# The fifth group of a down projection by seven products, and a reordered tail

## The chip, the cores and the metric

The kernel runs on one core of a Trainium2 chip. A core has a matrix engine (TensorE, in the profile PE, with its weight loads as PEld), a vector engine (DVE), a scalar engine (ACT), GpSimd (POOL) and SyncE (SP, which issues most DMAs). Each works through its own queue; they meet through semaphores. The metric is the time of one execution on the device in microseconds, the median of several runs.

## The reference

One encoder layer in float32, 512 rows of 1024 values. What bears on the change is its second half: a gated feed-forward part, whose down projection has a contraction of 2816 = 22 chunks of 128, and an embedding gate with a norm before and after it.

```python
    h2 = rmsnorm(x, norm_ffn_g[i])
    up = jnp.einsum('bsd,df->bsf', h2, w_up[i])
    up = causal_depthwise_conv(up, conv_w[i], conv_b[i])
    act = jax.nn.gelu(up[..., :D_FF]) * up[..., D_FF:]
    x = x + jnp.einsum('bsf,fd->bsd', act, w_down[i])

    h3 = rmsnorm(x, norm_ple_g[i])
    ple = jnp.einsum('bse,ed->bsd', p[i], w_ple[i])
    x = x + ple * jax.nn.sigmoid(jnp.einsum('bsd,de->bse', h3, w_ple_gate[i]))
return rmsnorm(x, norm_final_g)
```

## The kernel before

**Matmuls.** Every float32 product is made of three matmuls on float32r parts: an operand is split into a rounded high part and a low part (the rest), and low x high, high x low and high x high are summed in one PSUM bank. A matmul has a 128 x 128 stationary operand and a moving one of 128 x 512.

**Weights.** `load_w` (line 145) loads a piece of 512 KB into one of three raw buffers with a DMA from SP, casts it to the high part on ACT (line 153) and makes the low part in one of two ways: a subtraction on DVE (line 159), or, with "dma", a negated copy on ACT (line 156) and a DMA from GpSimd that adds the raw piece to it in place (line 157). The parts go to a ring of five pairs and one extra pair, so that a piece waits for the matmuls of the piece six before it. `split_w` (line 262) does the DVE way for weights that are in SBUF already.

**The up projection.** Eleven pairs of chunks, q = 0 to 10. For each, `up_jobs` (line 1332) has two jobs, gate and linear: 48 matmuls each, a convolution, the gelu or the product. The result goes to `done` (line 1437).

**The down projection by seven products.** Four chunks (two pairs q) make a group: 2 x 2 blocks of rows (256 each), of the contraction (256) and of columns (512), multiplied by seven products instead of eight. `pair_parts` (line 1311) makes the row-side operands of a pair, A11, A12, A22 and four sums S1 to S4, and their high and low parts, in a tile of one of the slots 2, 3, 5 and 7. `down_jobs(g)` (line 1367) loads the group's four weight blocks into slot 4, combines them in place, and makes the products in four jobs: A11 and S2; A12 and S1; S4 and S3; A22. Each product is 12 matmuls. Results are added to x1, the rows of the running sum, by DVE (line 1394); what A11 gives is needed in all four quarters and is gathered over the groups in `usum` (line 1401), and added to three quarters at the end (line 1467). `N_SEVEN` = 4 groups cover chunks 0 to 15.

**Order.** The list `jobs` alternates up jobs and down jobs; a job's weights are prepared while the job before it runs. The order in the text is binding for TensorE and SP in the sections marked `manual_schedule`; the other engines' order is set by a planner that runs through the program in simulated time and takes, of the instructions that are ready, the earlier one in the text.

**The last chunks and the tail.** Chunks 16 to 21 are projected plainly: the first column half for all four row blocks with six chunks (72 matmuls, line 1476), the second half block by block (`pd`, line 1538). As a block's second half ends, `evac_x2` (line 1480) adds it to x1, sums the squares and makes the norm: `rms_rows` (line 460) with a square root on ACT (line 391), four small DVE instructions and two scaled halves (line 468). `rest[rb]` then transposes that block (line 421) and splits it into h3T (lines 380, 381). The gate projection `pg` follows, 24 matmuls a block and column half, with its weights in pieces of two chunks. Two gain rows (lines 1472, 1473) go to slot 5 and the embedding rows `ple` (line 1477, 2 MB) to slot 4, when these are free. At the end `evac_gate` makes sigmoid, product, sum and the final norm, and the rows are stored.

Of the kernel before, what the change touches and what calls it, by code (L numbers as in the profile page):

```python
# [43 lines left out]
def hybrid_block(  # L44
# [217 lines left out]
    def split_w(raw):  # L262
        hi, lo = split_tiles(2, 512)
        A.copy(hi, raw)  # L264
        V.tensor_tensor(lo, raw, hi.bitcast(F32), ALU.subtract)  # L265
        return hi, lo
# [1038 lines left out]

    N_SEVEN = 4
    f_last, n_last = 4 * N_SEVEN, NF - 4 * N_SEVEN

    def pair_parts(e, o, t):
# [55 lines left out]
    def down_jobs(g):  # L1367
# [62 lines left out]

        def run3(ws):
            product(A22, ws[0], "z", add(2, 0))
        return [(ready0, run0), (ready1, run1), (ready2, run2), (lambda: (split_w(b21),), run3)]

    tiles = {}

    def done(q, i, uls):
        if q < 2 * N_SEVEN:
            if i:
                tiles[q] = slot((2, 3, 5, 7)[q % 4])  # L1440
                pair_parts(*uls, tiles[q])
            return
        if q == 2 * N_SEVEN and i == 0:
            tiles["last"] = tuple(k_view(slot(n), n_last) for n in (2, 3))
        split_out(tiles["last"], uls[i], (slice(None), 2 * q + i - f_last, slice(None)))

    jobs = up_jobs(0, done) + up_jobs(1, done)
    jobs[0] = (lambda: w_up0[0], jobs[0][1])
    jobs[1] = (lambda: w_up0[1], jobs[1][1])
    for g in range(N_SEVEN):  # L1450
        ups = up_jobs(2 * g + 2, done) + up_jobs(2 * g + 3, done)
        for pair in zip(ups, down_jobs(g)):
            jobs += pair
    jobs[2] = (lambda: up1, jobs[2][1])
    for q in range(2 * N_SEVEN + 2, NF // 2):
        jobs += up_jobs(q, done)

    with tc.manual_schedule(engines={ET.PE, ET.SP}):
        ws = jobs[0][0]()
        for n, (_, products) in enumerate(jobs):  # L1460
            nxt = jobs[n + 1][0]() if n + 1 < len(jobs) else None
            products(ws)
            ws = nxt
    for r in range(2):
        for rows, ch in ((0, 1), (2, 0), (2, 1)):
            t = x1[:, rows + r, 512 * ch:512 * ch + 512]
            V.tensor_tensor(t, t, usum[:, r, :], ALU.add)


    tail = slot(5, F32).rearrange("p (n c) -> p n c", n=4)  # L1470
    gple, gfin = tail[:, 0], tail[:, 1]
    nc.sync.dma_start(gple, rows_bc(norm_ple_g[0], D))
    nc.sync.dma_start(gfin, rows_bc(norm_final_g, D))
    ple = slot(4, F32).rearrange("p (b c) -> p b c", b=NB)
    f0, n, act = f_last, n_last, tiles["last"]
    proj_N(w_down_v, f0, n, act, 0, evac_x1a, rb_outer=False)
    nc.sync.dma_start(ple, ple_d.rearrange("(b q) c -> q b c", q=P))
    h3T = tuple(k_view(slot(i)) for i in (0, 1))

    def evac_x2(bk, rb, ch):  # L1480
        evac_x1(bk, rb, ch)
        ss1 = square_sum(bk, x1[:, rb, 512:], "s1")
        rest[rb] = rms_rows(x1[:, rb, :], half[rb], ss1, gple, scr, h3T, rb, tail[:, 2 + rb % 2])


    def add_ple(bk, rb, c):
# [47 lines left out]
            queue.dma_start(out_rows(rb, slice(0, D)), ple[:, rb, :])  # L1534
        rest[rb] = close

    with tc.manual_schedule(engines={mybir.EngineType.PE}):
        pd = proj_N_steps(w_down_v, f0, n, act, 1, evac_x2)
        steps(pd, 3 * n * 2 + 9)
        rest[0]()  # L1540
        steps(pd, 3 * n)
        rest[1]()
        steps(pd, 3 * n - 9)
        pg = proj_N_steps(w_pg_v, 0, NK, h3T, 0, evac_gate, subs=load_N(w_pg_v, 0, NK, 0, ("dma", "dma")))
        steps(pg, 20)
        rest[2]()
        steps(pg, 24)
        rest[3]()
        steps(pg, 52)
        subs = load_N(w_pg_v, 0, NK, 1, ("dma", "dma", None, None))  # L1550

# [60 lines left out]
```

## Time and profile before

| what | value |
|---|---|
| time, median of 3 runs (lowest, highest) | 932.3 us (931.84, 932.31) |
| the profiled execution | 932.14 us |
| its span, first to last instruction | 930.0 us |
| granted TensorE clock, mean | 0.997 |
| PE busy | 919.0 us, 99% |
| DVE busy, ACT busy | 634.8 us (68%), 556.4 us (60%) |
| matmuls | 4375 |

A row of instructions in order of time has the start in us from the span's start, the duration, the engine, the line, the operation and the tiles (out<-in). A row of the groups by line has the count, the busy time in us and the mean in ns, and behind the second bar the idle time of the engine before it and what ended it. Matmuls overlap: each is recorded with 0.39 us, and one starts every 0.23 us. "Issue to landing" of a DMA is the time from its issue to the last of its semaphore updates.

### The profile page before, as it was taken

How to read it: one execution, taken by the hardware profiler on the slowest of the kernel's cores; microseconds unless marked ns; L12 is line 12 of the kernel's file. 1: busy time of each engine (PE TensorE's matmuls, PEld its weight loads, DVE VectorE, ACT ScalarE, POOL GpSimd, SP SyncE). 2: the span in 40 equal slices, each digit the busy share in tenths (PEclk: the TensorE clock that was granted, in tenths of full speed). 3: DMA queues.
4: the chain of work that ended last, by engine and by line, in shares of the span. 5: the costliest groups of instructions: out<-in, count | busy, mean ns of one | idle time of the engine just before them, and what ended most of it. 6: DMA issues, size and time to landing. Idle time of an engine off the chain costs nothing.

```text
span 930.0 us, 12122 instructions
## 1 busy us (share of the span) xinstructions
PE 919.0 (99%) x4375; PEld 766.9 (82%) x4375; DVE 634.8 (68%) x1157; ACT 556.4 (60%) x891; POOL 102.6 (11%) x153
## 2 busy tenths in 40 slices
PE   9999999999999999999999999999999999999996
PEld 7878888888888888888888998888888888888885
DVE  5786899568777776634696747867676677464654
ACT  7754675477666677536556575756564645545633
POOL 1000000400000011000111010111110101100124
PEclk9999999999999999999999999999999999999998
DMA  9533264656444466499766496795675774975422
GB/s 338 193 93 113 81 185 121 235 140 166 117 115 122 117 163 153 167 364 323 178 202 117 136 205 183 169 251 116 155 205 128 225 167 101 236 239 136 116 66 91
DMA packets 109367, 156.36 MB, mean 168 GB/s; under 512 B 6132, under 2 KB 71852, under 8 KB 109308
## 3 DMA queue, kind: packets, MB, share of 16 engines
q1 hardware_dynamic: 96380, 110.73, 36.7%
q0 software_dynamic: 12784, 44.34, 24.2%
q8 instruction: 34, 0.56, 0.2%
q10 hardware_dynamic: 144, 0.52, 0.1%
q14 instruction: 25, 0.20, 0.1%
HBM read 105.74 MB, written 12.62 MB: 127 GB/s over the span
## 4 chain that ended last, share of the span: by engine, by line
PE 96%; DMA 1%; ACT 1%; DVE 1%; issue 0%; SPq 0%; DVEq 0%; POOLq 0%
PE bank L181 18%; PE bank L183 18%; PE bank L185 18%; PE bank L1387 8%; PE bank L1197 4%; PE bank L313 3%; PE bank L320 3%; PE bank L317 3%; PE bank L245 3%; PE bank L247 3%; PE bank L243 3%; PE bank L905 2%; PE bank L896 2%; PE bank L168 2%; PE bank L169 2%; PE bank L167 2%
## 5 line engine op out<-in xcount | busy, mean ns | idle before, releaser
L181 PE MATMUL bank<-slot,wlo 128*128 128x512 f32 (+1 forms) x696 | 272.6, 393 | 0.0
L183 PE MATMUL bank<-slot,whi 128*128 128x512 f32 (+1 forms) x696 | 267.3, 384 | 0.0
L185 PE MATMUL bank<-slot,whi 128*128 128x512 f32 (+1 forms) x696 | 266.9, 384 | 0.0
L185 PEld LDWEIGHTS bank<-slot,whi 128*128 128x128 f32 x696 | 130.9, 188 | 25.2
L181 PEld LDWEIGHTS bank<-slot,wlo 128*128 128x128 f32 x696 | 130.9, 188 | 20.7
L183 PEld LDWEIGHTS bank<-slot,whi 128*128 128x128 f32 x696 | 131.3, 189 | 19.4
L153 ACT CAST whi<-raw 128x1024 fp32r<-128x1024 f32 x95 | 99.2, 1048 | 39.0 <-PE bank L185 13.5
L157 POOL DMA_DIRECT2D wlo<-raw x55 | 47.7, 868 | 532.0 <-ACT wlo L156 351.5
L159 DVE TENSOR_TENSOR wlo<-raw,whi 128x1024 fp32r<-128x1024 f32 x39 | 48.4, 1244 | 27.5 <-ACT whi L153 27.0
L156 ACT ACTIVATE wlo<-whi 128x1024 fp32r<-128x1024 f32 x55 | 58.0, 1059 | 1.0
L1387 PE MATMUL bank<-whi,slot 128*128 128x512 f32 x176 | 56.5, 389 | 0.0
L245 PE MATMUL bank<-wlo,slot 128*128 128x512 f32 x106 | 41.7, 393 | 0.3 <-DVE wlo L159 0.2
L243 PE MATMUL bank<-whi,slot 128*128 128x512 f32 x106 | 41.7, 394 | 0.0
L878 ACT ACTIVATE t<-t,mn 128x512 f32<-128x512 f32 (+1 forms) x64 | 35.8, 560 | 9.7 <-DVE mn L875 8.3
L247 PE MATMUL bank<-whi,slot 128*128 128x512 f32 x106 | 41.5, 392 | 0.0
L1300 DVE SCALAR_TENSOR_TENSOR ul<-bank,cvT,ul 128x511 f32<-128x511 f32 x22 | 16.5, 750 | 36.5 <-ACT ul L1299 36.5
L1387 PEld LDWEIGHTS bank<-whi,slot 128*128 128x128 f32 x176 | 33.0, 188 | 6.9
L264 ACT CAST whi<-slot 128x1024 fp32r<-128x1024 f32 x22 | 23.0, 1044 | 23.8 <-PE bank L185 11.6
L1299 ACT ACTIVATE ul<-bank,cvT 128x512 f32<-128x512 f32 x22 | 17.1, 776 | 32.6 <-PE bank L185 32.6
L1300 DVE SCALAR_TENSOR_TENSOR ug<-bank,cvT,ug 128x511 f32<-128x511 f32 x22 | 16.4, 747 | 26.7 <-ACT ug L1299 26.6
L265 DVE TENSOR_TENSOR wlo<-slot,whi 128x1024 fp32r<-128x1024 f32 x22 | 26.9, 1221 | 11.0 <-ACT whi L264 11.0
L1387 PE MATMUL bank<-wlo,slot 128*128 128x512 f32 x88 | 34.2, 389 | 0.0
(368 smaller groups left out, 1913.7 us busy)
## 6 DMA issues: line engine op xcount, KB each, us to landing
wlo<-raw POOLq DMA_DIRECT2D x55, 512.0 KB, 5.3
raw<-in_w_up_dram SPq DMA_DIRECT2D x44, 512.0 KB, 5.2
raw<-in_w_in_dram SPq DMA_DIRECT2D x36, 512.0 KB, 3.9
more<-in_w_in_dram SPq DMA_DIRECT2D x20, 512.0 KB, 6.9
slot<-in_w_down_dram SPq DMA_DIRECT2D x16, 512.0 KB, 6.3
raw<-in_w_branch_b_dram SPq DMA_DIRECT2D x8, 512.0 KB, 3.9
slot<-in_w_out_dram SPq DMA_DIRECT2D x4, 1024.0 KB, 9.4
raw<-in_w_branch_a_dram SPq DMA_DIRECT2D x8, 512.0 KB, 7.1
```

The lines of the kernel that those rows point to most:

```text
L153: A.copy(hi, raw)
L156: A.activation(lo, hi.bitcast(F32), AF.Copy, scale=-1.0)
L157: G.dma_start(lo, raw, accum_op=ALU.add)
L159: (sub or V).tensor_tensor(lo, raw, hi.bitcast(F32), ALU.subtract)
L181: T.matmul(out_ap, wl, ah, start=(n == 0 and k == 0), stop=False)
L183: T.matmul(out_ap, wh, al, start=False, stop=False)
L185: T.matmul(out_ap, wh, ah, start=False, stop=end)
L243: T.matmul(bk, alo[:, k, r], wh, start=(k == 0), stop=False)
L245: T.matmul(bk, ahi[:, k, r], wl, start=False, stop=False)
L247: T.matmul(bk, ahi[:, k, r], wh, start=False, stop=(k == nk - 1))
L1197: T.matmul(bk, l, m, start=(fresh and q == 0 and n == 0), stop=(q == 3 and n == 2), skip_group_check=not fresh)
L1387: T.matmul(bk, l, m, start=(fresh and k == 0 and n == 0), stop=(k == 1 and n == 2), skip_group_check=not fresh)
```

## The change

`N_SEVEN` becomes 5: chunks 16 to 19 are a fifth group, and two chunks, 20 and 21, are left for the plain projection. The fifth group's first two jobs alternate with the last up pair as in the other groups. Its second half goes into `last_rows`: S3 and S4 (they end the upper rows' sums), then the plain chunks of both column halves for row blocks 0 and 1, then A22 (which ends the lower rows' sums), then the plain chunks for blocks 2 and 3. S3 stands before S4, where it stood behind it. The norms are taken apart into `norm_y` (the factor) and `norm_x2` (the scaled rows); both factors of a row half stand before the first block's rows. A small activation loads the square root's table ahead. The plain chunks' weights now go the "dma" way, and so do three of the four gate pieces, which are prepared one by one between these steps; the fourth is subtracted on DVE. The last pair's parts are in slot 7. The gain rows' loads are now in the section in which SP's order is that of the text; the `ple` load stands behind `last_rows`. PSUM banks are named in turn by two short lists. Transposes of blocks 0 and 1 stand before and after the last six plain matmuls, those of blocks 2 and 3 after 22 and 44 gate matmuls (before: 20 and 44).

```diff
--- before.py
+++ after.py
@@ -1305,7 +1305,7 @@
-    N_SEVEN = 4
+    N_SEVEN = 5
     f_last, n_last = 4 * N_SEVEN, NF - 4 * N_SEVEN
 
     def pair_parts(e, o, t):
@@ -1430,9 +1430,19 @@
 
         def run3(ws):
             product(A22, ws[0], "z", add(2, 0))
+        if g == N_SEVEN - 1:
+
+            def rows01(ws):
+                product(S3, ws[1], "z", add(2, 1))
+                product(S4, ws[0], "y", add(0, 1))
+
+            def rows23(w):
+                product(A22, w, "z", add(2, 0))
+            end.update(ready=ready2, rows01=rows01, ready23=lambda: split_w(b21), rows23=rows23)
+            return [(ready0, run0), (ready1, run1)]
         return [(ready0, run0), (ready1, run1), (ready2, run2), (lambda: (split_w(b21),), run3)]
 
-    tiles = {}
+    tiles, end = {}, {}
 
     def done(q, i, uls):
         if q < 2 * N_SEVEN:
@@ -1441,46 +1451,92 @@
                 pair_parts(*uls, tiles[q])
             return
         if q == 2 * N_SEVEN and i == 0:
-            tiles["last"] = tuple(k_view(slot(n), n_last) for n in (2, 3))
+            t = slot(7)
+            tiles["last"] = k_view(t, n_last), k_view(t[:, 512 * n_last:], n_last)
         split_out(tiles["last"], uls[i], (slice(None), 2 * q + i - f_last, slice(None)))
 
     jobs = up_jobs(0, done) + up_jobs(1, done)
     jobs[0] = (lambda: w_up0[0], jobs[0][1])
     jobs[1] = (lambda: w_up0[1], jobs[1][1])
-    for g in range(N_SEVEN):
+    for g in range(N_SEVEN - 1):
         ups = up_jobs(2 * g + 2, done) + up_jobs(2 * g + 3, done)
         for pair in zip(ups, down_jobs(g)):
             jobs += pair
+    for pair in zip(up_jobs(2 * N_SEVEN, done), down_jobs(N_SEVEN - 1)):
+        jobs += pair
     jobs[2] = (lambda: up1, jobs[2][1])
-    for q in range(2 * N_SEVEN + 2, NF // 2):
-        jobs += up_jobs(q, done)
-
-    with tc.manual_schedule(engines={ET.PE, ET.SP}):
-        ws = jobs[0][0]()
-        for n, (_, products) in enumerate(jobs):
-            nxt = jobs[n + 1][0]() if n + 1 < len(jobs) else None
-            products(ws)
-            ws = nxt
-    for r in range(2):
-        for rows, ch in ((0, 1), (2, 0), (2, 1)):
+
+    f0, n = f_last, n_last
+    proj = [None, None]
+
+    def evac_x2(bk, rb, ch):
+        evac_x1(bk, rb, ch)
+        sums[rb] = square_sum(bk, x1[:, rb, 512:], "s1")
+
+    def norm_y(rb):
+        V.tensor_tensor(half[rb], half[rb], sums[rb], ALU.add)
+        return rstd_of(half[rb], 1.0 / D)
+
+    def norm_x2(rb, y):
+        hn = tail[:, 2 + rb % 2]
+        for c in (slice(0, 512), slice(512, D)):
+            V.scalar_tensor_tensor(hn[:, c], x1[:, rb, c], y, gple[:, c], ALU.mult, ALU.mult)
+        rest[rb] = lambda: transpose_split(hn, h3T, rb)
+
+    pg_w = []
+
+    def pg_weights(j, sub):
+        pg_w.append(load_w(w_pg_v[:, 2 * j:2 * j + 2, 0:512], 2, 512, sub))
+
+    def add_usum(rows, ch):
+        for r in range(2):
             t = x1[:, rows + r, 512 * ch:512 * ch + 512]
             V.tensor_tensor(t, t, usum[:, r, :], ALU.add)
 
-
-    tail = slot(5, F32).rearrange("p (n c) -> p n c", n=4)
-    gple, gfin = tail[:, 0], tail[:, 1]
-    nc.sync.dma_start(gple, rows_bc(norm_ple_g[0], D))
-    nc.sync.dma_start(gfin, rows_bc(norm_final_g, D))
-    ple = slot(4, F32).rearrange("p (b c) -> p b c", b=NB)
-    f0, n, act = f_last, n_last, tiles["last"]
-    proj_N(w_down_v, f0, n, act, 0, evac_x1a, rb_outer=False)
-    nc.sync.dma_start(ple, ple_d.rearrange("(b q) c -> q b c", q=P))
-    h3T = tuple(k_view(slot(i)) for i in (0, 1))
-
-    def evac_x2(bk, rb, ch):
-        evac_x1(bk, rb, ch)
-        ss1 = square_sum(bk, x1[:, rb, 512:], "s1")
-        rest[rb] = rms_rows(x1[:, rb, :], half[rb], ss1, gple, scr, h3T, rb, tail[:, 2 + rb % 2])
+    def last_rows(ws):
+
+        w23 = end["ready23"]()
+        for ch, evac in enumerate((evac_x1a, evac_x2)):
+            proj[ch] = proj_N_steps(w_down_v, f0, n, tiles["last"], ch, evac,
+                                      subs=load_N(w_down_v, f0, n, ch, ("dma",)))
+        pg_weights(0, "dma")
+
+        A.activation(epst2, usum[:, 1, 0:1], AF.Sqrt, scale=0.0, bias=epst)
+        end["rows01"](ws)
+        state["turn"], state["bank"] = ["mm", "sc"], 0
+        steps(proj[0], 6 * n)
+        pg_weights(1, "dma")
+        steps(proj[1], 6 * n)
+        ys = [norm_y(rb) for rb in range(2)]
+        norm_x2(0, ys[0])
+        end["rows23"](w23)
+        norm_x2(1, ys[1])
+        pg_weights(2, "dma")
+        state["turn"], state["bank"] = ["mm", "sc", "mm", "pt", "pt", "sc", "mm", "pt"], 0
+
+    jobs.append((lambda: end["ready"](), last_rows))
+
+
+    def run_jobs(ws, n0, n1):
+        for n in range(n0, n1):
+            nxt = jobs[n + 1][0]() if n + 1 < len(jobs) else None
+            jobs[n][1](ws)
+            ws = nxt
+        return ws
+
+    with tc.manual_schedule(engines={ET.PE, ET.SP}):
+        ws = run_jobs(jobs[0][0](), 0, len(jobs) - 1)
+        tail = slot(5, F32).rearrange("p (n c) -> p n c", n=4)
+        gple, gfin = tail[:, 0], tail[:, 1]
+        nc.sync.dma_start(gple, rows_bc(norm_ple_g[0], D))
+        nc.sync.dma_start(gfin, rows_bc(norm_final_g, D))
+        h3T = tuple(k_view(slot(i)) for i in (0, 1))
+    with tc.manual_schedule(engines={ET.PE}):
+        for rows, ch in ((0, 1), (2, 1), (2, 0)):
+            add_usum(rows, ch)
+        last_rows(ws)
+        ple = slot(4, F32).rearrange("p (b c) -> p b c", b=NB)
+        nc.sync.dma_start(ple, ple_d.rearrange("(b q) c -> q b c", q=P))
 
 
     def add_ple(bk, rb, c):
@@ -1534,18 +1590,23 @@
             queue.dma_start(out_rows(rb, slice(0, D)), ple[:, rb, :])
         rest[rb] = close
 
-    with tc.manual_schedule(engines={mybir.EngineType.PE}):
-        pd = proj_N_steps(w_down_v, f0, n, act, 1, evac_x2)
-        steps(pd, 3 * n * 2 + 9)
+    with tc.manual_schedule(engines={ET.PE}):
+        pg = proj_N_steps(w_pg_v, 0, NK, h3T, 0, evac_gate, subs=pg_w)
+        steps(proj[0], 6 * n)
+        steps(proj[1], 3 * n)
         rest[0]()
-        steps(pd, 3 * n)
+        steps(proj[1], 3 * n)
         rest[1]()
-        steps(pd, 3 * n - 9)
-        pg = proj_N_steps(w_pg_v, 0, NK, h3T, 0, evac_gate, subs=load_N(w_pg_v, 0, NK, 0, ("dma", "dma")))
-        steps(pg, 20)
+        state["turn"], state["bank"] = BANK_TURN, 1
+        ys = [norm_y(rb) for rb in (2, 3)]
+        norm_x2(2, ys[0])
+        pg_weights(3, None)
+        norm_x2(3, ys[1])
+        steps(pg, 22)
         rest[2]()
-        steps(pg, 24)
+        steps(pg, 22)
         rest[3]()
+    with tc.manual_schedule(engines={ET.PE}):
         steps(pg, 52)
         subs = load_N(w_pg_v, 0, NK, 1, ("dma", "dma", None, None))
 
```

## The prediction

> **What bounds the kernel now.** I read the page first (busy times, the chain by engine), then the chain of waits in order of time over the last 170 us, then busy time by stage, and last the engines' own order in time around the edit. The page's head and its chain:
>
> ```profile
> span 930.0 us, 12122 instructions
> PE 919.0 (99%) x4375; PEld 766.9 (82%) x4375; DVE 634.8 (68%) x1157; ACT 556.4 (60%) x891; POOL 102.6 (11%) x153
> PE 96%; DMA 1%; ACT 1%; DVE 1%; issue 0%; SPq 0%; DVEq 0%; POOLq 0%
> ```
>
> PE is busy for 99% and is 96% of the chain, so the kernel is as long as its matmuls, and what matters is how many there are and whether one of them ever waits. Busy time by stage (columns: stretch, its length, PE, PEld, DVE, ACT, POOL with counts, granted clock, DMA share, GB/s):
>
> ```profile
> 740.00:760.00 20.00, 20.00 (x90) 16.56 (x89) 15.21 (x22) 12.06 (x16) 3.37 (x4) 1.00 0.69 187
> 850.00:900.00 50.00, 49.92 (x237) 41.38 (x236) 26.72 (x52) 29.24 (x52) 9.69 (x11) 1.00 0.50 116
> 861.48:877.72 16.24, 16.24 (x81) 13.61 (x80) 10.85 (x28) 10.11 (x19) 0.86 (x1) 1.00 0.39 100
> 900.00:930.00 30.00, 21.48 (x118) 18.59 (x116) 12.74 (x34) 9.61 (x21) 12.77 (x28) 0.92 0.18 70
> ```
>
> In the loop of seven-product groups (740 to 760) PE never waits although DVE is busy for 15.2 of 20 us. In the tail, where the edit is, DVE has much room: 10.85 of 16.24 us between 861.48 and 877.72. The last 8 us are the final norm and store, which the edit doesn't touch. The chain of waits, start, length, what:
>
> ```profile
> 767.60 5.44 PE bank L1387 x24
> 783.92 5.44 PE bank L1387 x24
> 800.24 5.44 PE bank L1387 x24
> 816.56 2.72 PE bank L1387 x12
> 867.57 0.87 PE bank L421 x8
> 875.28 4.54 DMA wlo<-raw
> ```
>
> The first four rows are the fourth group: 84 matmuls, 5.44/24 = 0.2267 us each. From its end, 819.28, 96 up-projection matmuls, 72 of the first output half and 45 of the second put the first transposes at 819.28 + 213 x 0.2267 = 867.57, which is the fifth row to the hundredth: nothing waits there, and positions may be computed by counting. The last row is the one wait in the tail. PE's own rows there:
>
> ```profile
> 879.40 0.39 PE L243 MATMUL bank<-whi,slot 128*128 128x512 f32 x1
> 879.87 0.50 PE L245 MATMUL bank<-wlo,slot 128*128 128x512 f32 x1
> ```
>
> The second starts 0.47 after the first instead of 0.23: 0.24 us lost to the low part of the last gate weight piece.
>
> **The change part by part.**
>
> *Matmuls removed.* Chunks 16 to 19 of the down projection took 4 chunks x 4 row blocks x 2 halves x 3 terms = 96 matmuls; as a fifth group they take 7 x 2 x 2 x 3 = 84. Twelve fewer, all on the path: 12 x 0.2267 = **-2.72 us**. Everything else PE does (transposes, gate) keeps its count.
>
> *Position of the rest.* From 819.28: 96 + 48 matmuls of the last up projection and the group's first two steps, so S3 starts at 851.92; S4 ends at 857.36; plain chunks, rows 0 and 1: 860.08 and 862.80 (block 0 complete at 861.44, as before); A22 ends at 865.52; then two blocks to 868.24, block 2 to 869.60, transposes of block 0 (0.87), block 3 to 871.83, transposes of block 1 to 872.70, and the gate starts there. Its fourth weight piece is first read after 18 matmuls, 876.78, and the transposes of block 2 stand after 22, 877.69.
>
> *Parts at nothing.* The operands of tiles 8 and 9 are now built by the pair routine and its seven weight splits and four combinations, more DVE and ACT work in 819 to 852; the cover is the same as in the row 740 to 760, where that very pattern leaves PE at 20.00 of 20. S3 now follows S1 at once and needs a bank that the A12 eviction frees; A12 ends 2.72 us earlier and an eviction is 0.69 (below), so without cover at most 0.7. The Sqrt table load comes off block 0's chain; that buys slack, not time. The two gain loads stand in SP's order behind the last up loads and the four new loads; they waited for the fourth group's end before too and are needed some 45 us later:
>
> ```profile
> 800.14 0.37 SPq L1477 DMA_DIRECT2D slot<-ple_d  x1
> 811.44 0.37 SPq L150 DMA_DIRECT2D raw<-in_w_up_dram  x1
> 818.63 0.34 SPq L1472 DMA_DIRECT2D slot<-in_norm_ple_g_dram  x1
> ```
>
> The 2 MB ple load moves most: its slot now holds the fifth group's weights until the last of them is split. That split's buffer is released at 843.76 (three quarters through the last linear half), so with a cast of 1.05 and a subtraction of 1.24 the load can go from about 846.1. DMA rows for 800 to 820, when it ran before, and for 841 to 866:
>
> ```profile
> DMA packets 2247, 5.51 MB, mean 275 GB/s; under 512 B 126, under 2 KB 829, under 8 KB 2246
> wlo<-raw POOLq DMA_DIRECT2D x3, 512.0 KB, 8.0
> ...
> raw<-in_w_ple_gate_dram SPq DMA_DIRECT2D x5, 512.0 KB, 3.3
> wlo<-raw POOLq DMA_DIRECT2D x2, 512.0 KB, 4.9
> ```
>
> At 275 GB/s its 2.1 MB take 7.6 us; it is needed at about 880. But it now overlaps the accumulating transfers of the plain chunks' weights, which took 4.9 us alone and 8.0 beside it. Before, the same step ran at the same moment for a gate piece:
>
> ```profile
> 846.52 1.05 ACT L153 CAST whi<-raw 128x1024 fp32r<-128x1024 f32 x1 [0.70 <-PE bank L169]
> 847.61 1.06 ACT L156 ACTIVATE wlo<-whi 128x1024 fp32r<-128x1024 f32 x1
> 848.96 0.86 POOL L157 DMA_DIRECT2D wlo<-raw  x1 [26.67 <-ACT wlo L156]
> ```
>
> The first plain piece's buffer is free at 846.48, so it can follow these rows: landing at 848.96 + 8.0 = 856.96, needed at 857.36 + 0.23 = 857.59. Zero, with 0.6 us of cover; one more ACT instruction ahead of it (0.78) makes it 0.2. The second piece follows 2.72 later on both counts. I take 0.
>
> *The gate weights.* Three pieces go by accumulating transfer as before, the fourth is now subtracted on DVE. Their raw buffers follow one another at a distance of three: the piece before last starts when a plain piece has landed (about 857 to 860), plus 3.3, 2.1 of ACT and 4.9, that is 867 to 871, against 874.3 and 875.7. The 0.24 us wait goes: **-0.24**.
>
> *The norm chains.* This is the term in doubt. The same DVE that had 5.4 us free now gets more between 861.48 (block 0 complete) and 877.69 (transposes of block 2). Groups of DVE in the tail (count, total, mean ns):
>
> ```profile
> L468 DVE SCALAR_TENSOR_TENSOR slot<-slot,ry,slot 128x512 f32<-128x512 f32 x8 | 5.6, 747 | 0.1
> L381 DVE TENSOR_TENSOR slot<-bank,slot 128x512 fp32r<-128x512 f32 x6 | 4.1, 684 | 0.8 <-ACT slot L380 0.7
> L1171 DVE TENSOR_TENSOR slot<-bank,slot 128x512 f32<-128x512 f32 x4 | 2.7, 687 | 4.1 <-PE bank L247 4.1
> L393 DVE TENSOR_SCALAR rt<-ry,ra 128x1 f32<-128x1 f32 x4 | 1.1, 273 | 0.1
> L394 DVE TENSOR_SCALAR ry<-rt,ry 128x1 f32<-128x1 f32 x4 | 0.8, 211 | 0.1
> L392 DVE RECIPROCAL ry<-rsd 128x1 f32<-128x1 f32 x4 | 0.6, 161 | 2.6 <-ACT rsd L391 2.6
> L463 DVE TENSOR_TENSOR s<-s,s 128x1 f32<-128x1 f32 x4 | 0.6, 158 | 2.7 <-ACT bank L457 2.7
> L386 DVE TENSOR_SCALAR ra<-s 128x1 f32<-128x1 f32 x4 | 0.6, 154 | 0.1
> ...
> L159 DVE TENSOR_TENSOR wlo<-raw,whi 128x1024 fp32r<-128x1024 f32 x39 | 48.4, 1244 | 27.5 <-ACT whi L153 27.0
> ```
>
> What must be done in those 16.2 us: 8 evictions (6 of the plain chunks, 2 of A22) x 0.687 = 5.5; 4 transposed low parts x 0.684 = 2.7; three norms' five small instructions, 0.957 each, 2.9; their scaled rows, 6 x 0.747 = 4.5; the fourth gate piece, 1.24. Sum 16.8, or 0.6 more than there is; block 3's small instructions, ahead of block 2's scaled rows in the text, make it 17.8, 1.5 too much. Against that, DVE instructions that follow each other start before the recorded end of the last:
>
> ```profile
> 865.33 1.42 DVE L468 SCALAR_TENSOR_TENSOR slot<-slot,ry,slot 128x512 f32<-128x512 f32 x2
> 866.66 0.69 DVE L1171 TENSOR_TENSOR slot<-bank,slot 128x512 f32<-128x512 f32 x1
> ...
> 875.36 0.30 ACT L391 ACTIVATE rsd<-s,epst 128x1 f32<-128x1 f32 x1
> ...
> 876.72 0.15 DVE L392 RECIPROCAL ry<-rsd 128x1 f32<-128x1 f32 x1
> ```
>
> The eviction starts 0.09 before the pair's end; over some 19 long instructions that is 1.5 us back. So by amount DVE is just full, with nothing left for waits; the lower end is 0 (no gain is possible beyond PE's count). And waits there are: the reciprocal at 876.72 had its input at 875.66 and came 1.06 later, behind others of the queue. Behind the norm instructions stand the evictions and low parts that the transposes and the gate need, so one such wait now reaches PE, late first at 876.78 or 877.69. I take 1.5 - 1.5 + 1.06, rounded to **+1.0**; the upper end is 1.5 without overlap and two waits, 3.6.
>
> *Sum.* The profiled execution took 932.14, its span of 930.0 and 2.14 around it; the median of the runs is 932.3, 0.16 more, which I leave out. 932.14 - 2.72 - 0.24 + 1.0 = **930.2 us**.
>
> **The rivals.**
>
> *DVE keeps up.* The planner places the fourth gate piece early (its buffer is free at 865.52) and each norm as its square arrives. For it: the stretch with 15.21 of 20 us of DVE above never stalls PE, and there are 8 us between block 0's end and its transposes, where 6.1 sufficed. Against it: no room in the sum. 932.14 - 2.96 = 929.2.
>
> *DVE becomes the bound.* Text order puts the fourth piece's subtraction behind block 2's rows; both are due within 0.9 us. With 1.5 and one wait of 1.06 the stall is 2.6: 931.8, no change that can be told. For it: the reciprocal's row; against it: the overlap. [...]
>
> *The ple load ahead of the plain weights.* SP issues in order. If the ple load stands there before the first plain piece, that piece isn't issued until 846.5 and lands behind 2 MB: 2.6 MB at 275 GB/s, 856.0; cast and negation 2.1 and 4.9 for the accumulation, 863.0; PE waits at 857.59 for 5.4 us: 929.2 + 5.4 = 934.6, slower. It decides from 4.8 us of stall on. For it: in the rows the ple load went at 800.14, before an up piece that the text names earlier. Against it: that piece then waited for a buffer, and the plain piece's buffer is free some 18 us before 846. [...]
>
> **How the numbers follow.** A measurement of this kernel can tell about 0.2% (1.9 us) from no change, so faster means under 930.4. The forecast, 929.7 to 930.9, has 0.38; DVE keeping up 0.27; DVE as the bound 0.23; the late plain weights 0.12. Faster: 0.27 and seven tenths of 0.38, 0.54. Slower: 0.12. The rest, 0.34, is the same. The range goes from 928.9 (no stall, and the runs' spread of 0.3) to 932.6 (a stall of 3.4, nearly the upper end); outside are the third rival and a little of the second.
>
> **What would show it.** Right: 12 fewer PE matmuls; S3 at 851.9; transposes of block 0 at 869.6; DVE busy for over 14 of the 16 us up to 877.7; PE's waits there put down to DVE rows or to the fourth gate piece, together near 1 us; the wait for the low part gone. Wrong: DVE with more than 2 us free there; a wait at 857.6 for the plain weights; PE waits over 2 us; or stalls in the group's loop before 851.

## The result, and the profile after

The kernel became slower: 938.42 us (937.8 to 938.61, 4 runs) against 932.07 us (931.61 to 932.31) for the kernel before on the same chip, a ratio of 1.0067 with a 95% interval of 1.0054 to 1.0079. The profiled execution took 938.61 us, its span is 936.8, 6.8 longer than before. The page of the kernel after, its head and the chain by engine:

```profile
span 936.8 us, 12146 instructions
PE 919.6 (98%) x4363; PEld 766.3 (82%) x4363; DVE 654.8 (70%) x1189; ACT 562.2 (60%) x900; POOL 103.9 (11%) x154
PE 93%; DMA 3%; ACT 1%; DVE 1%; issue 1%; SPq 0%; DVEq 0%; ACTq 0%; POOLq 0%
```

The twelve matmuls are gone (4363 for 4375), but PE's busy time is longer all the same, and its share of the chain fell from 96% to 93%: something else now sets the pace for a while, and some matmuls take longer. Where, the stretches tell (columns as in the prediction; kernel after):

```profile
740.00:760.00 20.00, 20.00 (x90) 16.58 (x89) 15.23 (x23) 12.03 (x15) 2.57 (x3) 1.00 0.69 188
850.00:900.00 50.00, 44.77 (x199) 36.52 (x198) 31.06 (x63) 27.63 (x50) 9.02 (x11) 0.93 0.69 180
861.48:877.72 16.24, 12.92 (x54) 10.30 (x53) 9.96 (x23) 8.20 (x16) 1.71 (x2) 0.90 0.84 227
```

The loop is what it was. In the tail PE loses 5 of 50 us, the granted clock falls to 0.90, and DVE, which the prediction thought full, has 9.96 us of work in 16.24. PE's longest waits (total, times, longest), and PE's rows in order of time:

```profile
PE bank L421 <- DVE slot L1483: 3.3, 1, 3.3
PE bank L451 <- DMA S1h<-in_p_dram: 1.9, 2, 1.2
PE bank L243 <- DVE slot L381: 1.9, 1, 1.9
```

```profile
870.04 0.39 PE L247 MATMUL bank<-whi,slot 128*128 128x512 f32 x1
873.75 1.78 PE L421 MATMUL bank<-ident,slot 128*128 128x128 f32 x8 [3.31 <-DVE slot L1483]
875.17 0.78 PE L243 MATMUL bank<-whi,slot 128*128 128x512 f32 x1
...
876.17 0.63 PE L247 MATMUL bank<-whi,slot 128*128 128x512 f32 x1
876.60 0.63 PE L243 MATMUL bank<-whi,slot 128*128 128x512 f32 x1
...
880.77 0.47 PE L243 MATMUL bank<-whi,slot 128*128 128x512 f32 x1 [1.92 <-DVE slot L381]
...
882.29 0.63 PE L245 MATMUL bank<-wlo,slot 128*128 128x512 f32 x1
882.71 0.63 PE L247 MATMUL bank<-whi,slot 128*128 128x512 f32 x1
```

Up to 870.04 PE runs as counted. Then it waits 3.3 us ahead of block 0's transposes and 1.9 us at the gate's start, and after each wait one matmul starts every 0.43 us instead of 0.23, at a mean granted clock of 0.57 (874 to 878) and 0.50 (882 to 884): 11 matmuls lose 2.2 us so, and the eight transposes take 1.42 (873.75 to 875.17) instead of 0.87.

The 6.8 us of span add up thus. The wait at the start of the kernel is 1.9 where it was 0.9 and shifts all that follows by 0.83; it isn't the change's (it lies far ahead of the edit, and the kernels below had 0.5 to 1.6 there). The matmuls and the old low-part wait bring -2.72 - 0.24. The two waits cost 3.31 + 1.92. What is left, 6.8 - 0.83 + 2.96 - 5.23 = 3.7, is the half clock (2.2 + 0.55) and about 1 us that no row accounts for exactly; the first matmuls behind each wait start 0.3 to 0.6 us apart.

What the waits are made of is on ACT. Its rows there, kernel after, in order of time, with the idle time before and what ended it:

```profile
860.32 0.60 ACT L457 ACTIVATE bank<-slot 128x512 f32<-128x512 f32 x1 [5.38 <-DVE slot L1171]
...
864.39 1.05 ACT L153 CAST whi<-raw 128x1024 fp32r<-128x1024 f32 x1 [3.35 <-DMA raw<-in_w_ple_gate_dram]
...
867.86 0.59 ACT L457 ACTIVATE bank<-slot 128x512 f32<-128x512 f32 x1
...
870.04 0.46 ACT L391 ACTIVATE rsd<-s,epst 128x1 f32<-128x1 f32 x2
...
877.29 1.05 ACT L153 CAST xhi<-raw 128x1024 fp32r<-128x1024 f32 x1 [5.06 <-DMA raw<-in_w_ple_gate_dram]
...
879.33 0.57 ACT L380 CAST slot<-bank 128x512 fp32r<-128x512 f32 x1
```

The squares of blocks 0 and 1 (line 457) stand behind the casts of gate pieces (line 153), and the copies of the transposed block 0 (line 380), of which PE had made the first before 875.2, stand behind the cast of a weight piece for the second output half, which PE reads only in the gate's second half, over 20 us later. ACT did nothing out of order: it sat idle for 3.35 and 5.06 us in front of casts whose raw piece hadn't come. The square behind the first cast had its input from 861.64 on, when its eviction on DVE ended, and the copies behind the second had theirs by 875.2, for the last 2 of the 5.06 us. DVE waited with it:

```profile
868.61 0.16 DVE L1477 TENSOR_TENSOR s<-s,s 128x1 f32<-128x1 f32 x1 [2.88 <-ACT bank L457]
...
871.69 1.22 DVE L159 TENSOR_TENSOR wlo<-raw,whi 128x1024 fp32r<-128x1024 f32 x1
...
872.95 1.40 DVE L1483 SCALAR_TENSOR_TENSOR slot<-slot,ry,slot 128x512 f32<-128x512 f32 x2
```

Not all of the first wait is ACT's: ahead of block 0's scaled rows (line 1483) DVE does the subtraction of the fourth gate piece, so that about 1.2 of the 3.3 us is DVE's own order.

The chain of waits ties it to the loads (start, length, what):

```profile
850.45 7.45 DMA xlo<-raw
857.96 6.35 DMA raw<-in_w_ple_gate_dram
...
871.86 5.36 DMA raw<-in_w_ple_gate_dram
```

There are three raw buffers, and a plain piece holds its own until its accumulating transfer has landed. That transfer ran beside the 2 MB ple load and took 7.4 us; only then, at 857.96, could SP issue the next gate piece, and this took 6.35, where the prediction's row had 3.3. The later pieces follow from there.

What ran beside this raw load, the DMA views tell: first the queue of SP's loads (q1: packets, MB, share of 16 engines) and the later two accumulating transfers (median from issue to landing) from 842 to 858, then the same queue from 857 to 870.

```profile
q1 hardware_dynamic: 528, 2.10, 37.3%
wlo<-raw POOLq DMA_DIRECT2D x2, 512.0 KB, 8.1
```

```profile
q1 hardware_dynamic: 816, 1.57, 33.5%
```

By 858 the whole ple load (2.10 MB) has passed, and from 855 on hardly a packet of it moves; the 1.57 MB that follow are three raw pieces. So this raw load didn't run beside the ple load, but beside the two accumulations issued at 852.51 and 855.23, which took 7.9 and 8.4 us, and from 860.4 on beside the next raw load. What the ple load slowed is the accumulation that held the buffer.

So the theory: late raw loads stand at the head of ACT's queue and hold up the norm chain and the transposed copies. The rivals: the ple load in itself; the clock at half; DVE short of time, as predicted; the fifth group itself.

### The profile page after: what moved, and what is told of

It reads as the page before. It is cut to its first block, busy times and chain, and to the rows that moved or that the text cites. A ratio compares the mean times of both kernels' runs of the same rounds, so it can differ in the third digit from the quotient of the medians.

```text
span 936.8 us, 12146 instructions
## 1 busy us (share of the span) xinstructions
PE 919.6 (98%) x4363; PEld 766.3 (82%) x4363; DVE 654.8 (70%) x1189; ACT 562.2 (60%) x900; POOL 103.9 (11%) x154
## 4 chain that ended last, share of the span: by engine, by line
PE 93%; DMA 3%; ACT 1%; DVE 1%; issue 1%; SPq 0%; DVEq 0%; ACTq 0%; POOLq 0%
PE bank L181 18%; PE bank L183 18%; PE bank L185 18%; PE bank L1387 9%; PE bank L1197 4%; PE bank L313 3%; PE bank L317 3%; PE bank L320 3%; PE bank L245 2%; PE bank L243 2%; PE bank L247 2%; PE bank L905 2%; PE bank L896 2%; DMA raw<-in_w_ple_gate_dram 1%; PE bank L168 1%; PE bank L169 1%
## 5 line engine op out<-in xcount | busy, mean ns | idle before, releaser
L181 PE MATMUL bank<-slot,wlo 128*128 128x512 f32 (+1 forms) x688 | 269.5, 393 | 0.0
L183 PE MATMUL bank<-slot,whi 128*128 128x512 f32 (+1 forms) x688 | 264.2, 384 | 0.0
L185 PE MATMUL bank<-slot,whi 128*128 128x512 f32 (+1 forms) x688 | 263.8, 384 | 0.0
L153 ACT CAST whi<-raw 128x1024 fp32r<-128x1024 f32 x91 | 95.2, 1048 | 32.2 <-PE bank L185 11.9
L1387 PE MATMUL bank<-whi,slot 128*128 128x512 f32 x232 | 74.2, 389 | 0.0
L159 DVE TENSOR_TENSOR wlo<-raw,whi 128x1024 fp32r<-128x1024 f32 x36 | 44.7, 1246 | 25.9 <-ACT whi L153 25.4
L1387 PEld LDWEIGHTS bank<-whi,slot 128*128 128x128 f32 x232 | 43.6, 188 | 9.0
L264 ACT CAST whi<-slot 128x1024 fp32r<-128x1024 f32 x29 | 30.2, 1045 | 30.5 <-PE bank L185 15.5
L1387 PE MATMUL bank<-wlo,slot 128*128 128x512 f32 x116 | 45.1, 389 | 0.0
L265 DVE TENSOR_TENSOR wlo<-slot,whi 128x1024 fp32r<-128x1024 f32 x29 | 35.4, 1220 | 13.3 <-ACT whi L264 13.3
L1394 DVE TENSOR_TENSOR slot<-bank,slot 128x512 f32<-128x512 f32 x60 | 40.6, 683 | 5.2 <-PE bank L1387 4.9
L243 PE MATMUL bank<-whi,slot 128*128 128x512 f32 x98 | 39.7, 405 | 1.9 <-DVE slot L381 1.9
L245 PE MATMUL bank<-wlo,slot 128*128 128x512 f32 x98 | 39.7, 405 | 0.2 <-DVE wlo L159 0.2
L247 PE MATMUL bank<-whi,slot 128*128 128x512 f32 x98 | 39.4, 402 | 0.0
```

The source lines that it names most:

```text
L159: (sub or V).tensor_tensor(lo, raw, hi.bitcast(F32), ALU.subtract)
L181: T.matmul(out_ap, wl, ah, start=(n == 0 and k == 0), stop=False)
L183: T.matmul(out_ap, wh, al, start=False, stop=False)
L185: T.matmul(out_ap, wh, ah, start=False, stop=end)
L243: T.matmul(bk, alo[:, k, r], wh, start=(k == 0), stop=False)
L245: T.matmul(bk, ahi[:, k, r], wl, start=False, stop=False)
```

## The experiments

All ratios are to the kernel before on the same chip, with their 95% intervals.

**e1_ple_late.** The ple load behind the four gate pieces, SP in text order.

```diff
         pg_weights(3, None)
+        ple = slot(4, F32).rearrange("p (b c) -> p b c", b=NB)
+        nc.sync.dma_start(ple, ple_d.rearrange("(b q) c -> q b c", q=P))
```

> One edit: the 2 MB ple load is issued behind the four gate pieces of the first half, and SP keeps the text's order there. Theory A (the squares of blocks 0 and 1 stand on ACT behind casts of gate pieces whose loads land late, 864.3 instead of about 859, because the ple load slows the plain pieces' accumulating transfers to 7.4 and 7.9 us and so holds back the raw buffers): those transfers fall back to about 5 us, the second gate piece's load goes at about 855.5, ACT no longer sits idle for 3.35 us before its cast, and of the 3.3 + 1.9 us of PE waits and the about 3 us at half clock most goes: 930 to 933. Rival B (DVE is simply full between 861 and 878, the forecast's term): DVE's work is unchanged, so nothing moves by more than 1 us: 937.5 to 939.

Measured 938.36 us, ratio 1.0058 [1.0042, 1.0075]. PE's waits, and ACT's row ahead of the long one:

```profile
PE bank L243 <- ACT bank L457: 5.6, 1, 5.6
PE bank L421 <- ACT bank L457: 0.6, 1, 0.6
```

```profile
878.88 1.04 ACT L153 CAST xhi<-raw 128x1024 fp32r<-128x1024 f32 x1 [4.23 <-DMA raw<-in_w_ple_gate_dram]
879.84 0.59 ACT L457 ACTIVATE bank<-slot 128x512 f32<-128x512 f32 x1
```

The ple load does delay the first gate pieces: without it SP went on at 854.97 instead of 857.96, and the wait ahead of the transposes shrank from 3.3 to 0.6. But the piece for the second half then comes behind the ple load, and its cast holds up ACT just as before. What PE waits for there is no copy (block 0's were made at 873.60) but a PSUM bank: the gate's first matmul takes the bank in which ACT writes the square of 879.84, and that stood behind the cast. Moving the 2 MB only moves the stall; the ple load alone isn't the cause.

**e2_plain_dve.** The plain pieces' low parts by subtraction on DVE, as before the change, so that they no longer hold a raw buffer through an accumulating transfer.

```diff
-                                      subs=load_N(w_down_v, f0, n, ch, ("dma",)))
+                                      subs=load_N(w_down_v, f0, n, ch))
```

> One edit: the low parts of the two plain pieces are subtracted on DVE instead of added by a transfer; two more DVE instructions of 1.24 us. Theory A: the raw buffers come free at about 850 to 853 instead of 857.96, the gate pieces land before 861 although the ple load runs, and the wait of ACT goes: 930 to 933. Rival B: 2.5 us more for a full DVE, so no faster than the changed kernel, 938 to 941.

Measured 930.85 us (929.72 to 931.21), ratio 0.9984 [0.9974, 0.9993]: some 7.5 us less than the change, from one argument that differs. PE's longest wait, the stretch up to block 2's transposes, and SP's queue:

```profile
PE bank L243 <- ACT bank L457: 1.3, 1, 1.3
```

```profile
861.40:877.60 16.20, 14.91 (x74) 12.31 (x73) 13.09 (x30) 12.04 (x26) 1.34 (x2) 1.00 0.80 205
```

```profile
850.83 26.48 SPq L150 DMA_DIRECT2D raw<-in_w_ple_gate_dram  x7
```

The next gate piece is issued 7 us earlier, the squares are on time, the clock stays at 1.00, and DVE does 13.09 us of work in the stretch, more than in the kernel after. That speaks for the late raw loads and against DVE as the bound. The edit also takes two negations (1.06 us each) off ACT and two accumulations out of the DMA queues; e5, which leaves both, separates part of this. The 1.3 us that remain are again a wait for a bank with a square in it (ACT at 873.57), ahead of which ACT casts a second-half piece (872.62, 1.05 us).

**e5_act_order.** The loads left late, but ACT in text order with the casts, those of the second half's first two pieces too, behind the squares and copies that PE needs first.

```diff
-    with tc.manual_schedule(engines={ET.PE}):
+    with tc.manual_schedule(engines={ET.PE, ET.Activation}):
...
+        splits[1]()
         steps(proj[1], 3 * n)
         rest[0]()
+        pg_weights(3, None)
+        splits[2]()
```

> One edit in several places: ACT takes the text's order in the tail, and in the text the casts of gate pieces 2, 3 and 4 and of the second half's first two pieces stand behind the squares, square roots and transposed copies that used to stand behind them. Transfers and the ple load stay as they are. Theory A: squares run as soon as the evictions are done, block 0's rows are scaled by about 867, PE's wait of 3.3 us at the first transposes goes, and so does the second one of 1.9 us; a wait of up to 1 us for the third gate piece's low part may come in its place: 929.5 to 932. Rival B: DVE's list is unchanged, 937 to 939. If the order on ACT matters less than the late transfers themselves: 933 to 937, with waits for gate pieces.

Measured 932.9 us, ratio 1.0005 [0.9996, 1.0015]. SP's issue is as late as in the kernel after (857.18), yet PE waits 2.3 us at the gate's start and under 1 us for the weights themselves:

```profile
PE bank L243 <- DVE slot L381: 2.3, 1, 2.3
PE bank L245 <- DMA wlo<-raw: 0.6, 1, 0.6
```

The time lies between the forecasts of the theory and of the third case. So both halves of the theory count: with late loads, the order on ACT is worth 5.5 us, the half clock included, which is gone in this profile (mean granted clock 0.997, in the kernel after 0.992). The rest to e2, 2.05 us, is no clean price of the late loads, since e5 also moves the second half's pieces and e2 leaves ACT's order to the planner.

**e4_warm.** Fourteen more matmuls, whose result is not used, ahead of the first transposes, to fill the wait.

```diff
+        keep = bank("av")
+        for _ in range(14):
+            T.matmul(keep, h2T[0][:, 0, 0:P], h2T[0][:, 0, :], start=True, stop=True)
         rest[0]()
```

> One edit: 14 matmuls of 128x512 on an unused bank, whose results nothing reads, just ahead of the transposes of block 0, where PE waited 3.3 us (14 x 0.227 = 3.2 us). Theory C (the wait of 3.3 us lowers the granted clock and 14 or so later matmuls took 0.43 instead of 0.23 us, about 3 us in all): the clock stays at 1.00 from 870 to 890 and the time falls by 2 to 3 us, to 935.5 to 936.5. Rival (the matmuls after the wait are slow for another reason, operands arriving late): the time stays at 938 or rises.

Measured 938.53 us, ratio 1.0066 [1.0051, 1.0081], as the kernel after. PE's rows:

```profile
868.92 3.49 PE L1599 MATMUL bank<-slot 128*128 128x512 f32 x14
...
873.83 0.39 PE L245 MATMUL bank<-wlo,slot 128*128 128x512 f32 x1
...
879.94 0.80 PE L243 MATMUL bank<-whi,slot 128*128 128x512 f32 x1 [3.91 <-DVE slot L381]
880.53 0.63 PE L245 MATMUL bank<-wlo,slot 128*128 128x512 f32 x1
```

The matmuls behind the first transposes now run at the full rate (one every 0.23 us from 873.83 on), but the gate starts when ACT is done: 11.0 us behind the last matmul ahead of the filling (868.92 to 879.94), where the kernel after has 10.5 behind the same matmul (870.27 to 880.77). The second wait is longer, 3.9 us, and the rate behind it is low all the same (one matmul every 0.43 us from 880.53 to 884.79): theory C had the clock right at the first place and the time wrong. In these rows and in those of the kernel after, half rate stands behind the waits, and in e4 not at the first place, where the wait is filled; it costs about 2 us at the gate's start (ten intervals of 0.43 us in place of 0.23), and taking it away at the first place alone gains nothing.

**e8_second_half.** Only the second place mended: the second half's weights behind the transposes of blocks 2 and 3, and ACT in text order there.

```diff
-    with tc.manual_schedule(engines={ET.PE}):
+    with tc.manual_schedule(engines={ET.PE, ET.Activation}):
...
+        pg_weights(3, None)
...
         rest[2]()
+        subs = [load_w(w_pg_v[:, 0:2, 512:], 2, 512, "dma")]
         steps(pg, 22)
         rest[3]()
+        subs.append(load_w(w_pg_v[:, 2:4, 512:], 2, 512, "dma"))
```

> The changed kernel with only the second of the two places mended: casts of the second half's gate pieces behind the copies, ACT in the text's order there; plain pieces and the casts of the first half's pieces 2 and 3 as in the changed kernel. Theory A, two places that add up: the first wait (3.3 us at the transposes of block 0, cold clock after it) stays, the second one goes; 934 to 936. If the two are one chain, in which the first wait alone sets the gate's start: 937 to 938.5. If the second place alone sets it: 930 to 932.

Measured 938.82 us (937.2 to 940.36), ratio 1.0077 [1.0062, 1.0093].

```profile
PE bank L421 <- DVE slot L1483: 3.4, 1, 3.4
PE bank L243 <- DVE slot L381: 1.9, 1, 1.9
PE bank L243 <- ACT whi L153: 1.2, 1, 1.2
```

```profile
876.46 0.60 ACT L457 ACTIVATE bank<-slot 128x512 f32<-128x512 f32 x1 [1.55 <-DVE slot L1171]
```

The first wait stays. The second has the same size but another cause: no cast stands ahead of the copies any more, they now stand behind a square that waits for DVE. The gate starts 5.5 us after the first transposes (872.94 to 878.43), where e4, at the full clock in this stretch too, has 7.5 (872.44 to 879.94); so some 2 us are won there. They are lost again at the second half, where the weights moved back come too late (1.2 us, and 0.8 for a low part). This profile, of an execution of 937.2 us, has no half clock behind its waits (granted clock 1.00 from 860 to 872 and from 872 to 884); the other three took 938.46 to 940.36, and no trace shows theirs. What the second place is worth by itself e8 therefore leaves open; all three forecasts missed.

**e6_dve_order.** e2 with the edit of e8, and ACT in text order up to the end of the gate's first half.

> The plain pieces' low parts on DVE, as in the run that came out at 930.85, and besides the casts of the second half's first two gate pieces moved in the text behind the transposed copies of blocks 2 and 3, with ACT in the text's order there, so that a cast that waits for its load no longer stands ahead of squares and copies. Theory A (what is left of the loss is the same queueing on ACT at a second place): PE's wait of 1.3 us at the gate's first matmul goes, nothing takes its place, 929.0 to 929.8, which is the time before less 12 matmuls and a wait of 0.24. Rival (the remaining wait comes from DVE, which now has more work): 930.5 to 931.5 as without the edit.

Measured 934.06 us, ratio 1.0017 [1.0009, 1.0026]. Stretch and waits:

```profile
861.40:877.60 16.20, 14.72 (x73) 12.16 (x73) 14.12 (x38) 8.52 (x23) 0.11 (x1) 1.00 0.66 177
```

```profile
PE bank L243 <- DVE slot L381: 1.5, 1, 1.5
PE bank L243 <- ACT whi L153: 1.2, 1, 1.2
```

Both forecasts missed. The wait at the gate's start didn't go with the cast; it is 1.5 us and now ends with a low part on DVE, which is busy without a pause from 864.59 to 873.12. That is a wait of the kind that the prediction had, for DVE's list, near its size; the stretch has 14.12 of 16.2 us of DVE work. The rest is again the late second half.

**e10_relieve_dve.** e2, and the fourth gate piece's low part by accumulating transfer, which takes 1.2 us from DVE.

```diff
-        pg_weights(3, None)
+        pg_weights(3, "dma")
```

> One edit against the run with the plain pieces on DVE (930.85): the fourth gate piece's low part goes by an accumulating transfer, 1.24 us off DVE and 1.06 us more on ACT. If DVE's list sets the remaining wait of 1.3 us at the gate's first matmul, it falls to below 0.5 us, 929.5 to 930.2. If ACT's order does, where the cast of a second-half piece still stands ahead of block 2's square, nothing is gained: 930.7 to 931.7.

Measured 930.36 us, ratio 0.9981 [0.9972, 0.999]; the wait at the gate's start is half of that in e2, whose time it equals within the spread. Time and wait lie between the two forecasts, so that e10 doesn't decide between them; the wait is still for a bank with a square of ACT in it:

```profile
PE bank L243 <- ACT bank L457: 0.6, 1, 0.6
```

**e9_best.** e10 with ACT in text order in the gate section, the fourth gate piece at its head, and the second half's first weights behind the copies of block 1.

```diff
         rest[1]()
         state["turn"], state["bank"] = BANK_TURN, 1
+        subs = load_N(w_pg_v, 0, 4, 1, ("dma",))
         ys = [norm_y(rb) for rb in (2, 3)]
         norm_x2(2, ys[0])
```

> On top of the run with the plain pieces on DVE (930.85): the fourth gate piece's low part goes by an accumulating transfer, so DVE has 1.24 us less between 861 and 878, where it was busy for 13.1 of 16.2 us there; and ACT takes the text's order in the gate section, with the casts of the second half's first two gate pieces behind the copies of blocks 0 and 1 and not before the squares. Theory: the last PE wait, 1.3 us at the gate's first matmul, has both causes, a cast that waits for its load ahead of the squares on ACT and DVE's full list; with both gone less than 0.5 us is left, 929.2 to 930.0. If the second half's weights come too late again (they made two waits of 2.4 us in all when their casts stood still further behind): 931 to 932.5.

Measured 932.0 us, ratio 0.9998 [0.999, 1.0007], a miss. PE waited 1.6 us ahead of block 2's transposes; DVE's row says for whom:

```profile
878.93 0.16 DVE L392 RECIPROCAL ry<-rsd 128x1 f32<-128x1 f32 x1 [3.10 <-ACT rsd L391]
```

The square roots of blocks 2 and 3 stood behind 4.2 us of casts and negations: the same fault as in the change, made anew by hand.

**e11_roots_first.** As e9, the second half's weights behind the scaled rows of blocks 2 and 3.

```diff
         norm_x2(2, ys[0])
         norm_x2(3, ys[1])
+        subs = load_N(w_pg_v, 0, 4, 1, ("dma",))
```

> As e9_best, but the second output half's first weight pieces (their casts and negations, 4.2 us of ACT) stand behind the factors and scaled rows of blocks 2 and 3 instead of ahead of them, so that the square roots of blocks 2 and 3 don't wait for them. If ACT's order in time is what is left (theory), the wait of 1.6 us ahead of block 2's transposes, which in e9_best was due to the square root behind those casts, goes, and the span comes to 928.3 to 929.0 us (the span of before, 930.0, less 2.72 for the twelve matmuls, with 1.0 to 1.7 us of waits left), the time to 929.6 to 930.4. If instead the rival holds, that DVE's amount of work in this stretch sets the transposes (e9_best has 11.9 of 16.2 us there), the wait ahead of the transposes of block 2 stays above 1 us and the time at 931 to 932.

Measured 929.38 us (929.05 to 930.02, 6 runs) against 932.39, ratio 0.9967 [0.9955, 0.9979]: faster than the kernel before by more than a measurement's uncertainty, the lowest median of all, though its interval overlaps those of e2 and e10. Its longest wait in the tail, its stretch, and ACT's rows:

```profile
PE bank L243 <- DVE slot L381: 0.8, 1, 0.8
```

```profile
861.40:877.60 16.20, 15.44 (x77) 12.76 (x76) 14.12 (x40) 12.59 (x26) 1.72 (x2) 1.00 0.74 200
```

```profile
873.48 0.49 ACT L391 ACTIVATE rsd<-s,epst 128x1 f32<-128x1 f32 x2
873.86 1.05 ACT L153 CAST xhi<-raw 128x1024 fp32r<-128x1024 f32 x1
```

The roots go first, the cast follows without a wait, and the wait ahead of block 2's transposes is gone, as the theory said; the time is a little below its forecast. DVE is as full as in e6, 14.12 of 16.2, and PE waits only 0.8 us: the sum over the stretch doesn't set the wait. Some 2 us of it are here the scaled rows of blocks 2 and 3, which stand behind the gate's start. What stands ahead of it does count: with the fourth piece's subtraction on DVE the wait is 1.5 us (e6), without it 0.8 (e9 and e11).

**e7_group_alone and e7b_group_alone.** The other direction: the kernel before with the fifth group, and the old order of the tail. The diff is that of e7b; in e7 the transposes stand one matmul later.

```diff
-    N_SEVEN = 4
+    N_SEVEN = 5
...
-        steps(pd, 3 * n * 2 + 9)
+        steps(pd, 3 * n * 3 - 1)
         rest[0]()
         steps(pd, 3 * n)
         rest[1]()
-        steps(pd, 3 * n - 9)
+        steps(pd, 1)
```

> The kernel before with only the fifth group added: all its four steps in order, then the two plain chunks of both column halves in the old order, with their weights on DVE, each block's norm in one piece, transposes of block 0 after 18 and block 1 after 24 of the last 24 plain matmuls. Twelve matmuls fewer. Theory: the norm chain of block 0, which took 6.1 us before, has 2.7 us left, so PE waits about 3 to 4 us, and 2 more at the gate's start for the split of block 0; with clock losses after it 932 to 936. If a fifth group alone were enough: 929.5.

e7 measured 946.41 us, ratio 1.0154, and says little: its transposes of blocks 0 and 1 stood after 18 and 24 of the last 24 plain matmuls, where the two row buffers are already overwritten by blocks 2 and 3 (blocks 0 and 1 of the gate are computed from these rows, so e7 computes something else), and PE waited for these later norms.

> The kernel before with the fifth group alone and the old tail's order, transposes of block 0 after 17 and of block 1 after 23 of the last 24 plain matmuls, so that the scaled rows of blocks 0 and 1 are read before blocks 2 and 3 reuse their buffers (in the run of this name without a b they were overwritten, so blocks 0 and 1 of the gate were computed from the rows of blocks 2 and 3 and the transposes waited for these). Block 0's second half ends 11 matmuls, 2.5 us, before its transposes, and its chain took 6.1 us before: PE waits 3 to 4 us there, some 2 more at the gate's first matmul, and loses clock behind it: 933 to 937. If the fifth group alone were enough: 929.5.

e7b measured 936.86 us (935.57 to 937.41), ratio 1.0047 [1.0032, 1.0062]:

```profile
PE bank L421 <- DVE slot L468: 5.1, 2, 2.7
```

```profile
868.99 1.28 ACT L391 ACT_TABLE_LOAD   x1
```

The group without the new tail is slower too: with two chunks only, fewer matmuls stand between a block's end and its transposes, and the norm chain, with the table load in it, isn't covered. A gate piece plays a small part here too: block 0's root has its input at 868.04, but ACT is at a negation until 868.97 and loads the table after it. That the reordering of the tail is needed is therefore argued and not shown; that the fifth group isn't enough by itself is shown.

## Why the prediction was wrong

It said 930.2 us (928.9 to 932.6); measured was 938.42. Point by point:

- *Matmuls removed*, -2.72: right. 4363 matmuls, the loop without a stall, and the transposes of block 0 due at 869.6 + 0.83 of shift = 870.43, against a last matmul from 870.04 to 870.43.
- *Parts at nothing*: the plain weights were in time, as it said; no wait for them at 857.6. It checked when they are needed, not what they hold: a raw buffer each, and the next gate pieces behind it. It had the 8.0 us of an accumulation beside the ple load in its own rows, and used it for the plain piece only.
- *The gate weights*: here it failed. "The piece before last starts when a plain piece has landed (about 857 to 860)" was right (860.4, and 857.96 for the piece ahead of it), but "plus 3.3" was not: these two raw loads took 5.2 and 6.35 us. Worse, the step compared the result with the time at which PE reads the weights, and never asked what stands behind the casts in ACT's queue. It put their lateness at no cost; the runs show PE waits of 3.3 and 1.9 us in its place, of which the order on ACT made 5.5 us of time with the half clock behind them (e5), and holding the raw buffers 7.5 us (e2). The two prices overlap and are not to be added. For the rival of a full DVE it had named a reciprocal that came 1.06 us behind its input, behind others of DVE's queue, and it looked at that queue alone. The -0.24 was right and doesn't matter beside it.
- *The norm chains*, +1.0: not what happened. In the changed kernel DVE had 6 of 16.24 us free, which the prediction named as a sign against itself. With loads in time a wait of this kind appears, 1.5 us in e6 and 0.8 in e9 and e11, but it goes by what stands ahead of the gate on DVE and not by the sum of 16.8 us that the term was worked out from; the 1.3 us of e2 are ACT's and no support. That the size fits these runs is in part luck.
- *The rivals*: none is what came. "The ple load ahead of the plain weights" was nearest in kind and time (934.6), but SP issued the plain pieces first (at 813.71 and 828.30, the ple load at 846.97), and the stall lies 13 us later. The 934.6 is 929.2 and a single wait of 5.4 us. Measured were two waits, 3.31 and 1.92, and beside them 3.7 us, of which the matmuls and transposes at half rate behind each wait (0.43 us a matmul) make 2.75 and about 1 us isn't half clock; that the two waits together come near this rival's one is chance.

Still open is why the planner set the casts ahead of the squares: the trace shows the order, not its reasons; that it reckoned with earlier loads is only argued. Open, too, is what each wait costs alone: every run that moved one of them moved something else with it.

## What to carry to other kernels

When a step is given a transfer in place of an instruction, ask not only when its result is needed, but which buffer it holds meanwhile and which load that puts off. Then look at the engine that receives the late load: in the kernel after, ACT sat idle for 3.35 and 5.06 us in front of two casts whose raw piece hadn't come, and a square and the transposed copies, ready before these waits ended, came behind the casts. So instructions on the critical chain belong ahead of casts for later stages. And mend all such places of one chain together: in e1 the first wait shrank from 3.3 to 0.6 us, the next grew from 1.9 to 5.6, and the time stayed.

## What the hardware showed that was not expected

A raw load of 512 KB took 3.3 us in the kernel before (median of five) and 6.35 beside two accumulating transfers and, from 860.4 on, another raw load. Three accumulations in a row took 7.4, 7.9 and 8.4 us in the kernel after, the first two begun beside the 2 MB load, and 4.5, 5.7 and 7.5 in e1, without it. The ple load thus cost the first one 2.9 us; the rest of the rise comes without it. In the stretch up to 877.72 the DMA engines were busy for 0.84 of the time for 227 GB/s.

In the kernel after, a wait of 3.3 us and one of 1.9 us were each followed by half rate (one matmul every 0.43 us, at a granted clock of 0.57 from 874 to 878 and 0.50 from 882 to 884), while in the profile of e8 waits of 3.4 and 1.9 us left the granted clock at 1.00 from 860 to 872 and from 872 to 884. So the length of a wait alone doesn't tell whether half rate follows; what does, no run here shows.
